# Attention on one NeuronCore: odd heads with exchanged query halves, key blocks in falling order, and a mask product over 512 columns

## Chip, cores and metric

One core of one Trainium2 chip. The metric is the device time of one execution in microseconds (us); the times of the kernel before are from three runs, and the median counts. The profile is of one further execution. Engines are named as in the profile: PE (matrix products; PEld is its weight load), DVE (vector), ACT (scalar), POOL (here stores and small memsets), SP (issues the loads).

## What is computed

One step of a small decoder: 1024 prompt positions and 8 decode positions, model width 2048. Layer A is a pooling mixer, then keys and values are projected once (4 key heads of 64), then layer B is sliding-window attention with 32 query heads of 64, a gate and an output projection. The change touches the attention of the prompt in layer B only:

```python
def attn_core(q, k, v, q_pos, k_pos, sinks):
    s = jnp.einsum('...qkgd,...skd->...kgqs', q, k).astype(jnp.float32) * (HEAD_DIM ** -0.5)
    ...
    mask = (kp <= qp) & (qp - kp < WINDOW) & (kp >= 0)
    s = jnp.where(mask[..., None, None, :, :], s, NEG)
    sink = sinks.astype(jnp.float32).reshape(N_KV_HEADS, GROUP)[:, :, None, None]
    m = jnp.maximum(jnp.max(s, axis=-1, keepdims=True), sink)
    p = jnp.exp(s - m)
    p = p / (jnp.sum(p, axis=-1, keepdims=True) + jnp.exp(sink - m))
    return jnp.einsum('...kgqs,...skd->...qkgd', p.astype(v.dtype), v)
```

With a window of 128, query q of a block of 128 sees keys 0 to q of its own block and keys q+1 to 127 of the block before, exactly 128 keys in all.

## The kernel before

**Staging.** The columns (positions) are worked in two chunks of 512 and 520, all of them in SBUF tiles of 128 x 1040 float32. 53 such slots (class `Mem`) are shared by everything: weights, activations, probabilities, gates. A slot is handed out whole (`full`) or in halves (`half`), the one that has been free longest first. Which slot a tile gets, and so whose last reader it must wait for, is thus settled when the program is built, by the order of the requests and of the frees; so is the place of a load, because activations and some sums are loaded ahead only while enough whole slots are free.

**Big products.** Input and output projections run as triples of PE products on numbers split into a high and a low part (lines 658 to 660, seven products for eight by sums of halves; lines 686 to 688, plain). A weight chunk is loaded by SP (line 287), ACT casts its high part (line 488), DVE subtracts for the low part (line 503) or forms sums of two chunks (lines 293 and 346). Activations (written to DRAM earlier and loaded at line 759) are cast at 769 and subtracted at 778. Partial sums are put away at 599 to 631.

**Order.** PE, DVE and ACT follow the order of the source (`in_order`). The big products of one phase are the steps; `product(n, rank, ...)` puts a smaller product between them, `at(n, ...)` puts other work n steps on. SP has one queue for all loads and runs it strictly in order: a load whose slot is still in use holds every later load. POOL issues the stores.

**Attention** (`attend`, lines 1745 to 1901) runs for 16 pairs of heads (j = 0, 1) in each of the two chunks, 32 times in all, as steps between the products of the input projection of layer B. Queries come from a rope step (lines 1616 to 1731: partner rows are fetched by four DMAs at 1616, added at 1624, finished at 1731). For a pair, with b the block of 128 queries in the chunk:

- score (line 1760): 32 PE products of 64 queries by 192 keys, in PSUM tile `pS`; query half u of block b goes to partitions u to u+63 and columns b*256+u on. The columns never written are zeroed once (`use_four`).
- select (ACT, 1778; in chunk 0 a POOL memset at 1776) copies the 128 columns of the block before into a slot; largest (DVE, 1782) overwrites them by `copy_predicated` with the scores of the own block where the key is not after the query, so that one row of 128 holds the whole window; then the row maxima (1786 to 1790).
- expo (ACT, 1797): eight activations of 128x128, one for each block and head, each summing its row; total (DVE, 1804 and 1805): the reciprocal; norm (ACT, 1810): eight activations of 128x128 that scale.
- turn (PE, 1814): eight transposes of 128x128 into PSUM; keep: ACT copies the 128x1024 result into slot `w` (1823) and DVE multiplies the same 128x1024 by a triangular mask of 0, 1 and -1 into slot `wp` (1824).
- values (PE, 1848): for each half k of the 64 keys a product of `w` with the values of one of the two blocks (64x128), and a correction of 64x64 with the difference of the two blocks' values on `wp`. The correction reads only the half of the columns of `wp` that belongs to query half k.
- gate (DVE, 1876), and a store by POOL.

## Time and profile before

| | us |
|---|---|
| median of 3 runs | 2360.77 (2357.7 to 2366.27) |
| profiled execution, its own time | 2356.38 |
| its span in the trace | 2354.6 |
| PE busy | 2297.3 |
| DVE busy | 1925.9 |
| ACT busy | 1343.1 |
| POOL busy | 205.5 |

The first attention step begins at 1157.9 us of the span and the last ends before 2060. A row of a group reads: line, engine, operation, output and input with their shapes, xcount | busy us, mean ns of one | idle us of the engine just before, and what ended that idle time. A row of waits reads: engine, tile and line that waited, the work it waited for, then us in total, how often, the longest.

### The profile page before, as it was taken

What the parts mean: (1) busy time and instruction counts of PE and PEld (TensorE: products, weight loads), DVE (VectorE), ACT (ScalarE), POOL (GpSimd) and SP (SyncE); (2) the same over time, 40 slices, a digit from 0 to 9 for tenths busy, and PEclk for the clock granted to TensorE, in tenths of its full rate; (3) what the DMA queues carried; (4) which work ended last, traced back from release to release, by engine and by line L of the source; (5) the groups of instructions that cost most, each with busy time, mean ns of one, the idle gap of its engine ahead of it and who ended that gap; (6) DMA issues with size and microseconds to landing.
All of it is one profiled execution on the core that took longest, in us unless ns stands there. A gap on an engine that the chain in (4) does not pass through costs nothing. (4 is left out here: it accounts for less than half of the span.)

```text
span 2354.6 us, 49710 instructions
## 1 busy us (share of the span) xinstructions
PE 2297.3 (98%) x19960; PEld 2200.9 (93%) x19960; DVE 1925.9 (82%) x2421; ACT 1343.1 (57%) x2429; POOL 205.5 (9%) x411
## 2 busy tenths in 40 slices
PE   8999999999999999999999899999999999999997
PEld 6899999999999999998788799999999999999997
DVE  8787998776878878978987788887777768888887
ACT  4444446544546547554465566685666678546556
POOL 0111110001000000000111111100000000000000
PEclk9999999999999999999999999999999999999999
DMA  8668789989889989999786766688777768799785
GB/s 293 211 246 303 271 299 346 332 292 319 289 289 339 327 280 333 328 388 327 272 310 220 248 219 239 224 310 270 237 249 245 230 201 305 239 342 372 260 300 199
DMA packets 250919, 665.18 MB, mean 283 GB/s; under 512 B 25632, under 2 KB 106432, under 8 KB 250688
## 3 DMA queue, kind: packets, MB, share of 16 engines
q1 hardware_dynamic: 205216, 496.94, 63.0%
q0 software_dynamic: 45472, 165.07, 18.1%
q8 instruction: 156, 2.56, 0.4%
q14 instruction: 75, 0.61, 0.1%
HBM read 466.81 MB, written 185.59 MB: 277 GB/s over the span
## 5 line engine op out<-in xcount | busy, mean ns | idle before, releaser
L658 PE MATMUL pD<-m,m 128*128 128x260 f32 (+1 forms) x4752 | 1346.0, 283 | 8.1 <-ACT pD L599 4.4
L660 PE MATMUL pD<-m,m 128*128 128x260 f32 (+1 forms) x4752 | 1339.1, 282 | 4.4 <-DVE m L503 4.4
L659 PE MATMUL pD<-m,m 128*128 128x260 f32 (+1 forms) x4752 | 1338.8, 282 | 0.0
L658 PEld LDWEIGHTS pD<-m,m 128*128 128x128 f32 x4752 | 894.5, 188 | 13.7 <-ACT pD L599 5.5
L660 PEld LDWEIGHTS pD<-m,m 128*128 128x128 f32 x4752 | 895.2, 188 | 5.5 <-DVE m L503 5.5
L503 DVE TENSOR_TENSOR m<-m,m 128x1024 fp32r<-128x1024 f32 x674 | 814.5, 1219 | 100.1 <-ACT m L488 60.6
L659 PEld LDWEIGHTS pD<-m,m 128*128 128x128 f32 x4752 | 894.9, 188 | 0.5
L488 ACT CAST m<-m 128x1024 fp32r<-128x1024 f32 x674 | 702.7, 1049 | 324.7 <-DVE m L346 85.1
L686 PE MATMUL pD<-m,m 128*128 128x512 f32 x448 | 179.7, 401 | 8.0 <-ACT m L769 8.0
L687 PE MATMUL pD<-m,m 128*128 128x512 f32 x448 | 177.9, 397 | 1.0 <-DVE m L778 1.0
L688 PE MATMUL pD<-m,m 128*128 128x512 f32 x448 | 177.5, 396 | 0.0
L778 DVE TENSOR_TENSOR m<-m,m 128x1024 fp32r<-128x1024 f32 (+1 forms) x120 | 147.0, 1226 | 6.4 <-ACT m L769 4.7
L769 ACT CAST m<-m 128x1024 fp32r<-128x1024 f32 (+1 forms) x120 | 125.9, 1053 | 17.7 <-PE pD L687 5.2
L631 ACT COPY m<-pD 128x260 f32<-128x260 f32 (+1 forms) x83 | 31.1, 375 | 179.2 <-PE pD L660 179.1
L346 DVE TENSOR_TENSOR m<-m,m 128x1024 f32<-128x1024 f32 x88 | 107.6, 1222 | 12.7 <-DMA m<-in_wib 6.3
L686 PEld LDWEIGHTS pD<-m,m 128*128 128x128 f32 x448 | 85.1, 190 | 28.1 <-ACT m L769 8.0
L687 PEld LDWEIGHTS pD<-m,m 128*128 128x128 f32 x448 | 85.0, 190 | 21.1 <-DVE m L778 2.1
L688 PEld LDWEIGHTS pD<-m,m 128*128 128x128 f32 x448 | 85.0, 190 | 19.7
L1797 ACT ACTIVATE m<-m,sm 128x128 f32<-128x128 f32 x256 | 99.4, 393 | 0.0
L619 DVE TENSOR_TENSOR m<-pD,m 128x260 f32<-128x260 f32 (+1 forms) x86 | 36.5, 424 | 74.4 <-PE pD L660 74.1
L1088 PE MATMUL pD<-m,m 128*128 128x260 f32 (+1 forms) x528 | 91.5, 323 | 0.0
L1088 PEld LDWEIGHTS pD<-m,m 128*128 128x128 f32 x528 | 79.5, 188 | 8.2
(249 smaller groups left out, 2180.9 us busy)
## 6 DMA issues: line engine op xcount, KB each, us to landing
m<-in_wia SPq DMA_DIRECT2D x124, 512.0 KB
m<-in_wib SPq DMA_DIRECT2D x120, 512.0 KB
swia<-m POOLq DMA_DIRECT2D x64, 512.0 KB, 4.8
m<-swia SPq DMA_DIRECT2D x64, 512.0 KB
m<-swoa SPq DMA_DIRECT2D x64, 512.0 KB
swib<-m POOLq DMA_DIRECT2D x64, 512.0 KB, 5.1
m<-swib SPq DMA_DIRECT2D x64, 512.0 KB
m<-swob SPq DMA_DIRECT2D x56, 512.0 KB
```

The lines of the kernel that those rows point to most:

```text
L346: self.nc.vector.tensor_add(s[out].a[:, :1024], s[x].a[:, :1024], s[y].a[:, :1024])
L488: self.nc.scalar.copy(hi.r[:, :1024], self.stream[self.cast].src().a[:, :1024])
L503: self.nc.vector.tensor_sub(lo.r[:, :1024], s.src().a[:, :1024], hi.a[:, :1024])
L658: nc.tensor.matmul(ps[:, :TH], wh[:, s], h, start=new and k == 0, stop=False, skip_group_check=on)
L659: nc.tensor.matmul(ps[:, :TH], wh[:, s], l, start=False, stop=False, skip_group_check=on)
L660: nc.tensor.matmul(ps[:, :TH], wl[:, s], h, start=False, stop=k == 7, skip_group_check=on)
L686: nc.tensor.matmul(ps[:], wh[:, s], h, start=par == 0 and k == 0, stop=False)
L687: nc.tensor.matmul(ps[:], wh[:, s], l, start=False, stop=False)
L688: nc.tensor.matmul(ps[:], wl[:, s], h, start=False, stop=par == 1 and k == 7)
L769: self.nc.scalar.copy(h.r[:, :n], s.a[:, :n])
L778: self.nc.vector.tensor_sub(l.r[:, :n], s.a[:, :n], h.a[:, :n])
L1088: nc.tensor.matmul(ps[:, : cs.stop - cs.start], ws[:, s], d[:, cs], start=f0 and k == 0, stop=l0 and k == 3,)
```

## The change

Which elements stand where is changed for the odd head of each pair, so that the two triangles that the correction needs lie in the same columns, one in partitions 0 to 63 and one in partitions 64 to 127.

- score: for j = 1 the two halves of 64 queries go to exchanged output partitions (z = 64-u). The 192 keys are read as three blocks of 64 in falling order, for both heads, so the own block lies in columns 0 to 127 of each 256 and the block before in 128 to 255. Number and shape of the products stay.
- select and largest take the other half of the columns; the mask of `copy_predicated` has a plane for each head, in bytes instead of 32-bit integers.
- norm: `wp` is now half a slot, taken at norm(0) instead of a whole slot at keep. The activations of blocks 0 and 7 are each cut in two of 64 columns, one of which writes into `wp`.
- turn: the transposes read 64 columns further on, so each result holds in its upper 64 partitions the second half of one block and in its lower 64 the first half of the next; the eighth reads the 128 columns in `wp`.
- keep: `w` as before; the product with the mask covers blocks 0 and 3 of each four, 512 columns, and is written over the same half slot `wp`.
- values: number and shape of the products stay; the index of the block of probabilities is turned by k, and for j = 1 the moving operand of the 64x128 products is read with its two halves exchanged.

```diff
-        self.mki = one.tile([P, P], I32, name="mki")
+        self.mki = one.tile([P, 2, P], U8, name="mki")
...
-                            self.S[u : u + 64, j, b * 256 + u : b * 256 + u + 192],
-                            q[r, b * P + u : b * P + u + 64],
-                            self.kT[t // 8][r, b * P + u : b * P + u + 192], start=True, stop=True,
+                            o.rearrange("p (m k) -> p m k", m=3), q[r, b * P + u : b * P + u + 64],
+                            k.rearrange("p (m k) -> p m k", m=3)[:, ::-1, :], start=True, stop=True,
...
-            nc.scalar.copy(s4[:, b0:], p4[:, b0:, :, 0:P])
+            nc.scalar.copy(s4[:, b0:], p4[:, b0:, :, P : 2 * P])
...
-                s4, self.mki[:, None, None, :].to_broadcast([P, NB, 2, P]), p4[:, :, :, P : 2 * P]
+                s4, self.mki[:, None, :, :].to_broadcast([P, NB, 2, P]), p4[:, :, :, 0:P]
...
+            if n == 0:
+                x["wp"] = self.mem.half()
             for i in range(4 * n, 4 * n + 4):
-                nc.scalar.activation(x["s3"][:, i, :], x["s3"][:, i, :], AF.Copy, scale=rs[:, i : i + 1])
+                v = x["s3"][:, i, :]
+                parts = [(v, v)]
+                if i in (0, 7):
+                    k1, k0 = v[:, :64], v[:, 64:]
+                    e = x["wp"].a[:, :P]
+                    parts = [(k0, k0), (e[:, 64:], k1)] if i == 0 else [(k1, k1), (e[:, :64], k0)]
+                for out, a in parts:
+                    nc.scalar.activation(out, a, AF.Copy, scale=rs[:, i : i + 1])
...
-                    PT[:, i * P : (i + 1) * P], x["sc"][:, i * P : (i + 1) * P], cst[:, K_ID : K_ID + P]
-                )
+                a = x["sc"][:, i * P + 64 : (i + 1) * P + 64] if i < 7 else x["wp"].a[:, :P]
+                nc.tensor.transpose(PT[:, i * P : (i + 1) * P], a, cst[:, K_ID : K_ID + P])
...
-            x["w"], x["wp"] = self.mem.full(), self.mem.full()
+            x["w"] = self.mem.full()
             nc.scalar.copy(x["w"].a[:, :1024], PT)
             nc.vector.tensor_mul(
-                x["wp"].a[:, :1024].rearrange("p (i k) -> p i k", k=P),
-                PT.rearrange("p (i k) -> p i k", k=P),
-                cst[:, None, K_MP : K_MP + P].to_broadcast([P, 8, P]),
+                x["wp"].a[:, :512].rearrange("p (b i k) -> p b i k", b=NB, i=2), mixed(slice(0, NB)),
+                cst[:, None, None, K_MP : K_MP + 64].to_broadcast([P, NB, 2, 64]),
             )
...
+                            i = (2 * b + j - k) % 8
...
+                                p = x["w"].a[r, i * P : i * P + P].rearrange("p (h q) -> p h q", h=2)
+                                if j:
+                                    p = p[:, ::-1, :]
```

**The order on SP.** Because `wp` is half a slot, most tiles after the first attention step get another slot, and some loads get another place in SP's queue. One place is the third phase of layer B's input projection, about 1300 to 1343 us in the trace of before. A row is line, DMA, slot with two running numbers <- DRAM tensor, shape; `in_wib` is the weight of layer B's input projection, `th0_92` an activation, line 1616 the rope partner rows. Before:

```order
L287 DMA m33_1722_14842<-in_wib 128x1024
L759 DMA m26_1729_14943<-th0_92 128x4x256
L287 DMA m45_1730_14945<-in_wib 128x1024
L759 DMA m2_1740_15039<-th0_92 128x4x256
L287 DMA m7_1731_14947<-in_wib 128x1024
L1616 DMA m40_1737_15030<-m43_1667_14239 32x512 x4
L759 DMA m50_1741_15041<-th0_92 128x4x256
L759 DMA m28_1747_15090<-th0_92 128x4x256
```

The same place after the change (line numbers are one higher there):

```order
L288 DMA m37_1718_14847<-in_wib 128x1024
L288 DMA m43_1724_14948<-in_wib 128x1024
L288 DMA m31_1725_14950<-in_wib 128x1024
L760 DMA m47_1734_15042<-th0_92 128x4x256
L760 DMA m0_1735_15044<-th0_92 128x4x256
L1617 DMA m33_1731_15033<-m3_1696_14596 32x512 x4
L760 DMA m9_1739_15090<-th0_92 128x4x256
L760 DMA m11_1740_15092<-th0_92 128x4x256
```

The three weight loads now stand together, and the two activation loads that stood between them follow behind.

**The order on ACT.** The place is the two norm steps of the first pair. `m_1605` is the slot with its probabilities, `sm` small vectors; 2050 to 2055 and 1908 (after: 2067 to 2072 and 1925) belong to the gate, 488 (489) is the cast of a weight. Before:

```order
L1810 ACTIVATE m_1605_13466<-m_1605_13466,sm_13487 128x128 x4
L2055 COPY m_1606_13496<-pD_13495 128x512
L1908 ACTIVATE m_1616_13600<-m_1606_13496 128x512
L488 CAST m_1619_13606<-m_1612_13552 128x1024
L1810 ACTIVATE m_1605_13466<-m_1605_13466,sm_13487 128x128 x4
```

After, where `m_1606` is `wp`:

```order
L1822 ACTIVATE m_1605_13466<-m_1605_13466,sm_13487 128x64
L1822 ACTIVATE m_1606_13496<-m_1605_13466,sm_13487 128x64
L1822 ACTIVATE m_1605_13466<-m_1605_13466,sm_13487 128x128 x3
L2072 COPY m_1589_13290<-pD_13495 128x512
L1925 ACTIVATE m_1616_13601<-m_1589_13290 128x512
L489 CAST m_1619_13607<-m_1612_13552 128x1024
L1822 ACTIVATE m_1605_13466<-m_1605_13466,sm_13487 128x128 x3
L1822 ACTIVATE m_1605_13466<-m_1605_13466,sm_13487 128x64
L1822 ACTIVATE m_1606_13496<-m_1605_13466,sm_13487 128x64
```

Each pair's norm has ten activations instead of eight, over the same columns. On PE the order of the rows stays as it was; on DVE the product with the mask keeps its place.

More of the change, by code (lines that the diff above doesn't have):

```diff
@@ L11 @@
 F32R = mybir.dt.float32r
-I32 = mybir.dt.int32
+U8 = mybir.dt.uint8
 AF = mybir.ActivationFunctionType
@@ L45 @@
 N_PRM = 116
-K_ID, K_MP, K_J, K_RC = 0, 128, 256, 384
-N_CST = 384 + 4 * NST
+K_ID, K_MP, K_J, K_RC = 0, 128, 192, 320
+N_CST = 320 + 4 * NST
 PHASES = (
@@ L248, in use_four @@
             for j in range(2):
-                self.nc.vector.memset(S4[64:, j, :, :64], 0.0)
-                self.nc.vector.memset(S4[:64, j, :, 192:], 0.0)
+                a, b = (slice(0, 64), slice(64, P))[:: 1 - 2 * j]
+                self.nc.vector.memset(S4[a, j, :, :64], 0.0)
+                self.nc.vector.memset(S4[b, j, :, 192:], 0.0)
     def psW(self):
@@ L1759, in score @@
                         r = slice(64 * j, 64 * j + 64)
+                        z = u if j == 0 else 64 - u
+                        o = self.S[z : z + 64, j, b * 256 + 64 - u : b * 256 + 256 - u]
+                        k = self.kT[t // 8][r, b * P + u : b * P + u + 192]
                         nc.tensor.matmul(
-                            self.S[u : u + 64, j, b * 256 + u : b * 256 + u + 192],
-                            q[r, b * P + u : b * P + u + 64],
-                            self.kT[t // 8][r, b * P + u : b * P + u + 192], start=True, stop=True,
+                            o.rearrange("p (m k) -> p m k", m=3), q[r, b * P + u : b * P + u + 64],
+                            k.rearrange("p (m k) -> p m k", m=3)[:, ::-1, :], start=True, stop=True,
                         )
@@ L1808, in norm, with mixed @@
             rs = x["sm"][3]
+            if n == 0:
+                x["wp"] = self.mem.half()
             for i in range(4 * n, 4 * n + 4):
-                nc.scalar.activation(x["s3"][:, i, :], x["s3"][:, i, :], AF.Copy, scale=rs[:, i : i + 1])
+                v = x["s3"][:, i, :]
[6 more added lines that the diff above has]
+                    nc.scalar.activation(out, a, AF.Copy, scale=rs[:, i : i + 1])
         def turn():
             for i in range(8):
-                nc.tensor.transpose(
-                    PT[:, i * P : (i + 1) * P], x["sc"][:, i * P : (i + 1) * P], cst[:, K_ID : K_ID + P]
-                )
+                a = x["sc"][:, i * P + 64 : (i + 1) * P + 64] if i < 7 else x["wp"].a[:, :P]
+                nc.tensor.transpose(PT[:, i * P : (i + 1) * P], a, cst[:, K_ID : K_ID + P])
             x["s"].free()
+        def mixed(b):
+            return PT.rearrange("p (b i k) -> p b i k", b=NB, i=4)[:, b, 0:4:3, :]
         def keep():
-            x["w"], x["wp"] = self.mem.full(), self.mem.full()
+            x["w"] = self.mem.full()
             nc.scalar.copy(x["w"].a[:, :1024], PT)
             nc.vector.tensor_mul(
-                x["wp"].a[:, :1024].rearrange("p (i k) -> p i k", k=P),
-                PT.rearrange("p (i k) -> p i k", k=P),
-                cst[:, None, K_MP : K_MP + P].to_broadcast([P, 8, P]),
+                x["wp"].a[:, :512].rearrange("p (b i k) -> p b i k", b=NB, i=2), mixed(slice(0, NB)),
+                cst[:, None, None, K_MP : K_MP + 64].to_broadcast([P, NB, 2, 64]),
             )
@@ L1842, in values @@
                         o = x["o"][b // 2]
-                        V, p = (self.Vd[b], x["wp"].a) if step else (self.V[b + 1 - k], x["w"].a)
-                        c0, c1 = (64 * k, 64 * k + 64) if step else (0, P)
+                        V = self.Vd[b] if step else self.V[b + 1 - k]
                         for j in range(2):
                             vs = slice((2 * (t // 8) + j) * HD, (2 * (t // 8) + j + 1) * HD)
-                            m = (2 * b + j) * P
+                            i = (2 * b + j - k) % 8
+                            out = o[64 * j : 64 * j + 64, n * P : (n + 1) * P].rearrange("p (h q) -> p h q", h=2)
+                            if step:
+                                out, p = out[:, k, :], x["wp"].a[r, i * 64 : i * 64 + 64]
+                            else:
+                                p = x["w"].a[r, i * P : i * P + P].rearrange("p (h q) -> p h q", h=2)
+                                if j:
+                                    p = p[:, ::-1, :]
                             ins = nc.tensor.matmul(
-                                o[64 * j : 64 * j + 64, n * P + c0 : n * P + c1], V[r, vs], p[r, m + c0 : m + c1],
+                                out, V[r, vs], p,
                                 start=part == 0 and n == 0 and step == 0, stop=part == 1 and step == 1,
@@ L2272, in _consts @@
     cst[:, K_ID : K_ID + P] = np.eye(P, dtype=f)
-    cst[:64, K_MP : K_MP + P] = i[:64, None] > i[None, :]
-    cst[64:, K_MP : K_MP + P] = -1.0 * (i[64:, None] <= i[None, :])
+    h = i[:64]
+    cst[:64, K_MP : K_MP + 64] = h[:, None] > h[None, :]
+    cst[64:, K_MP : K_MP + 64] = -1.0 * (h[:, None] <= h[None, :])
     cst[:, K_J : K_J + P] = 1.0 / D
@@ L2277, in _consts @@
         cst[:, K_RC + g * NST : K_RC + (g + 1) * NST] = w / np.minimum(w, np.arange(NST) + 1.0)
-    return cst, (i[None, :] <= i[:, None]).astype(np.int32)
+    k = (i + 64) % P
+    return cst, np.stack([k[None, :] <= q[:, None] for q in (i, k)], axis=1).astype(np.uint8)
 def kernel(**inputs):
```

## Prediction

> **What bounds the kernel now.** I read the page first, then the busy time by stretch, with the attention as the middle stretch.

> ```profile
> PE 2297.3 (98%) x19960; PEld 2200.9 (93%) x19960; DVE 1925.9 (82%) x2421; ACT 1343.1 (57%) x2429; POOL 205.5 (9%) x411
> 0.00:1157.00 1157.00, 1142.58 (x8696) 1099.72 (x8696) 952.38 (x1188) 580.42 (x822) 103.04 (x198) 1.00 0.86 304
> 1157.00:2060.00 903.00, 879.45 (x9019) 830.57 (x9020) 723.39 (x942) 587.99 (x1352) 85.01 (x185) 0.99 0.75 251
> ```

> The columns of a stretch are its us, then the busy us of PE, PEld, DVE, ACT and POOL, the granted PE clock, the DMA share and GB/s. PE is the bound: in the attention stretch it idles 903.0 - 879.5 = 23.5 us, while DVE idles 180 us and ACT 315 us. The change leaves number and shape of the PE products alone, so whatever it saves on DVE counts only where it shortens PE's 23.5 us of idle time, or the time PE ran at a lower clock. The next view is therefore what PE waits for in that stretch.

> ```profile
> PE pS L1760 <- DVE m L1731: 8.4, 8, 1.5
> PE pO L1848 <- ACT m L1823: 7.8, 1, 7.8
> PE pD L658 <- ACT pD L599: 1.8, 2, 0.9
> PE pS L1848 <- DVE m L1824: 1.5, 3, 0.7
> PE pD L660 <- DVE m L503: 1.3, 2, 1.1
> PE pD L1848 <- ACT m L614: 1.3, 1, 1.3
> PE pO L1848 <- DVE m L1824: 0.6, 1, 0.6
> ```

> Only two rows, 1.5 + 0.6 us, name the product with the mask, which is what the change shortens. The two large ones are the scores that wait for the rope step, and one single wait of 7.8 us. I followed that one back in time, engine by engine.

> ```profile
> 1311.58 0.38 SPq L759 DMA_DIRECT2D m<-th  x1
> 1312.06 0.45 SPq L287 DMA_DIRECT2D m<-in_wib  x1
> 1320.25 0.38 SPq L759 DMA_DIRECT2D m<-th  x1
> 1320.73 0.99 SPq L287 DMA_DIRECT2D m<-in_wib  x1
> SPq L759 <- DMA swib<-m: 7.7, 1, 7.7
> 1321.97 1.22 DVE L503 TENSOR_TENSOR m<-m,m 128x1024 fp32r<-128x1024 f32 x1
> 1328.94 1.22 DVE L346 TENSOR_TENSOR m<-m,m 128x1024 f32<-128x1024 f32 x1 [5.75 <-DMA m<-in_wib]
> 1330.20 1.04 ACT L488 CAST m<-m 128x1024 fp32r<-128x1024 f32 x1 [9.02 <-DVE m L346]
> 1333.73 1.00 ACT L1823 COPY m<-pS 128x1024 f32<-128x1024 f32 x1
> 1326.60 0.40 PE L688 MATMUL pD<-m,m 128*128 128x512 f32 x1
> 1334.79 0.48 PE L1848 MATMUL pO<-m,m 64*64 64x128 f32 x2 [7.79 <-ACT m L1823]
> 1336.05 0.37 PE L1848 MATMUL pO<-m,m 64*64 64x64 f32 x2 [0.55 <-DVE m L1824]
> ```

> On SP an activation load (759) stood 7.7 us until a store out of its slot (`swib`) was done, and held the weight load behind it until 1320.73. DVE had nothing to do from 1323.19 until the weight came (5.75 us), added it at 1328.94; ACT, which keeps the order of the source, stood at the cast of that sum and so came to the copy of the probabilities (1823) only at 1333.73; PE stood 7.79 us. The wait is put down to ACT, but its root is a load that came late. It also cost clock, in the windows around it:

> ```profile
> 1320.00:1327.00 7.00, 7.00 (x35) 5.45 (x33) 3.09 (x5) 0.59 (x1) 0.11 (x1) 1.00 0.97 298
> 1327.00:1335.00 8.00, 0.21 (x4) 0.21 (x8) 3.73 (x4) 4.80 (x14) 1.07 (x2) 0.71 0.98 269
> 1335.00:1341.00 6.00, 5.45 (x42) 4.15 (x39) 5.97 (x6) 2.23 (x9) 0.70 (x3) 0.53 0.95 302
> 1341.00:1350.00 9.00, 9.00 (x88) 8.00 (x87) 8.86 (x16) 7.50 (x15) 2.09 (x4) 1.00 0.85 319
> ```

> The granted clock was 0.53 from 1335 to 1341, just when PE had work again: 6.0 x (1 - 0.53) = 2.8 us more. So this one stall is worth 7.8 + 0.55 + 2.8 = 11 us.

> [...]

> **The change part by part.** First the product with the mask.

> ```profile
> L1824 DVE TENSOR_TENSOR m<-pS,cst 128x1024 f32<-128x1024 f32 x32 | 39.2, 1225 | 57.2 <-ACT m L1823 46.5 <-PE pD L659 9.0 <-ACT m L1810 1.8
> L1731 DVE TENSOR_TENSOR m<-m,m 128x512 f32<-128x512 f32 x8 | 5.5, 692 | 0.3
> 1820.74 1.23 DVE L1824 TENSOR_TENSOR m<-pS,cst 128x1024 f32<-128x1024 f32 x1 [0.91 <-ACT m L1823]
> 1822.13 2.39 DVE L1624 TENSOR_TENSOR m<-m,m 128x1040 f32<-128x1040 f32 x2
> 1824.56 1.24 DVE L1731 TENSOR_TENSOR m<-m,m 128x1040 f32<-128x1040 f32 x1
> 1481.23 1.22 DVE L1731 TENSOR_TENSOR m<-m,m 128x1024 f32<-128x1024 f32 x1
> L1624 DVE TENSOR_TENSOR m<-m,m 128x1040 f32<-128x1040 f32 x18 | 21.5, 1236 | 6.8 <-DMA m<-m 6.8
> L1782 DVE COPY_PREDICATED m<-mki,pS 128x1024 f32<-128x1024 int32 x32 | 42.2, 1320 | 0.0
> ```

> 1225 ns for 1024 columns and 692 ns for 512 give 0.53 us a pair, 32 x 0.53 = 17 us of DVE's busy time (the 512 columns are no longer in one piece in PSUM; nothing here shows a price for that). It cannot be 17 us of time: the mask product itself was preceded by 57.2 us of idle time, 46.5 of them for ACT's copy. What reaches PE is this. The values waits on 1824: four, 2.1 us, three of them in the 1.5 us row, of which at most 0.53 each can go: -1.3. The score waits on 1731: where DVE runs mask product, two rope adds and 1731 without a gap (the rows at 1820.74 to 1824.56 are one place; the 1731 at 1481.23 ends another such run, and there is a third at 1432), the 0.53 us come through whole: three times, -1.6. The other five of the eight are held by the partner rows' DMA (6.8 us of idle time before 1624). SP's queue before several of those DMAs moves forward in the changed order; between 0 and -3, I take -1.

> Second the slots. With `wp` as half a slot, the third phase's three weight loads stand together ahead of the two activations. Following the slots to their last readers: the second and third weights of the group take slots whose last readers are the PE products (686 to 688) that end with the activation load's own wait at 1311.58. So both should be issued by about 1312, 9 us sooner than 1320.73. The load took at most 1328.94 - 1320.73 = 8.2 us to land; from 1312 that is 1320.2, before DVE is free at 1323.19. DVE's sum then moves forward by the whole 5.75 us, ACT's copy behind it too, and PE's wait falls from 7.79 to about 2.0 us. At 2 us I expect no drop of the clock: PE's other waits here are at most 1.5 us, and none shows one. With the 0.55 mostly gone: -5.75 - 2.8 - 0.3 = -8.9 us. What is late next there is the ACT chain from the cast to the copy, unchanged. Ends: -5.7 if the clock still drops, -11 if the whole stall goes. What was pushed back, the activation loads and the sums that wait for spare slots, comes later by 6 to 65 us, and with before's times each still lands 6 us or more ahead of its use; that is the cover, and if one misses it, a wait like the one above returns (a rival).

> Third ACT's pieces.

> ```profile
> 1308.38 1.28 ACT L1810 ACTIVATE m<-m,sm 128x128 f32<-128x128 f32 x4
> L1810 ACT ACTIVATE m<-m,sm 128x128 f32<-128x128 f32 x256 | 82.3, 399 | 6.1 <-DVE sm L1805 6.1
> 1331.15 0.20 ACT L1795 ACTIVATE sm<-sm 128x8 f32<-128x8 f32 x1
> L1814 PE MATMUL pS<-cst,m x256: 270/272/274, 1200.4 to 2027.8; 128*128 128x128 f32 x128
> ```

> Four pieces take 1.28 us, so they follow (1.28 - 0.40) / 3 = 0.29 us apart. A piece of 64 columns lies between 128 x 8 (0.20 us long) and 128 x 128 (0.40), about 0.1 shorter than the latter: 0.19 apart. Two more pieces a pair then cost 4 x 0.19 - 2 x 0.29 = 0.18 us, 32 times 6 us; at the ends 0 (two halves cost as much as a whole) and 0.58 x 32 = 19 us. The cover is ACT's 315 idle us, and the transposes, which wait for norm, appear nowhere among PE's waits. New is that norm(0) waits for its half slot; `select` of another pair, casts and copies queue behind it. Where the slot has just been read by a product, I find three such waits of about 1.4 us, before idle stretches of ACT. I take +1 for all this, ends 0 and +5.

> [...]

> Fourth, PE's own products: same number, shapes and order. The moving operands are now read in pieces of 64 columns in falling order, which no row of before shows. I take nothing, since the columns within a piece stay in rising order; the price if that is wrong is a rival. `copy_predicated` with a byte mask reads less; it could be quicker than its 1.32 us (mean of the 32), and is hidden either way, as no PE wait names it. The memsets and constants are done once.

> Fifth, every slot after the first pair is another, so small waits come and go elsewhere: between -2 and +5, I take +1.

> Sum: -1.3 - 1.6 - 1 - 8.9 + 1 + 1 = -10.8, about -11 us. The profiled run took 2356.4 us (span 2354.6 and 1.8 around it), so it would take 2345.4. The median of the three runs is 4.4 us above the profiled one; on its scale the forecast is 2360.8 - 10.8 = 2350.

> **The rivals.**

> (a) The saving lies beside other work, and the stall stays or returns elsewhere as another late load. For it: 46.5 us of DVE's idle time is for ACT's copy, so the mask product is rarely late, and the sums for the next phase do move later. Against it: the order shows the very load moved ahead. It leaves -1.3 - 1.6 and up to +2: -1 to -4, so 2357 to 2360.

> (b) More goes than I count: the whole stall (11), all 8.4 us of score waits that DMA or DVE hold, and the values waits: -11 - 6 to 8 - 2 = -19 to -21, so 2340 to 2342. For it: DVE, which is ahead by up to 17 us in sum, releases slots sooner. Against it: the ACT chain at the stall, 4.5 us from cast to copy, is not shortened.

> (c) Slower: the moving operands in falling pieces of 64 columns are read more slowly. The place is score, and values for odd heads.

> ```profile
> 1351.14 1.53 PE L1760 MATMUL pS<-m,m 64*64 64x192 f32 x32
> ```

> Were each pass twice as long, a score would cost about 1.5 us more, 32 x 1.5 = 48 us all on PE, so 2350 + 48 = 2398. It decides from a lengthening of 23% on: 32 x 0.35 = 11 us eats the gain. Nothing in the trace speaks for it, nothing excludes it. A second way to this side, the half slot held from norm(0) on, which would bring an activation late enough for a stall of 11 us on top of the one that is there, would give 2369; I count it with (a), as still under 0.5%.

> (d) The change does not save what it says: 512 columns in two pieces of 128 for each block cost DVE as much as 1024. That only takes away 1.3 + 1.6: 2353.

> **How the numbers follow.** A measurement of this kernel can tell about 0.5% from no change, 11.8 us: faster is under 2349.0, slower over 2372.6. My forecast of -11 with its terms' ends (-6 to -15, with d in it) has a chance of 0.62, half on each side of 2349; (a) 0.20; (b) 0.12; (c) 0.06. Faster: 0.31 + 0.12 = 0.43; within: 0.31 + 0.20 = 0.51; slower: 0.06. The range goes from (b)'s 2340 to (a)'s 2360, with 1 us for the medians; it leaves out (c) and the tails of the others, 0.15 or so.

> **What would show it.** Right: SP issues the three weight loads of that place by about 1312; PE's wait there is near 2 us and the clock stays at 1.00; the mask product takes 0.69 us; DVE's busy time falls by 17 us while the span falls by 11; PE's busy time stays within 3 us (its half-clock stretch) of 2297; ACT's rises by 6. Wrong: a new PE wait of more than 3 us in 1157 to 2060, a score of over 1.6 us, or a second stretch of lower clock.

## The result

The median went from 2358.07 us to 2346.02 us, six runs each: a ratio of 0.9945, with a 95% interval of 0.9930 to 0.9961. That is 12 us less; the forecast was 10.8 us less, and 2350 on the scale of the three runs shown then. The profiled execution took 2346.26 us, its span is 2344.4 us, 10.2 less than before.

The busy times of the changed kernel, from its page:

```profile
PE 2297.8 (98%) x19960; PEld 2202.2 (94%) x19960; DVE 1908.6 (81%) x2421; ACT 1353.3 (58%) x2493; POOL 205.2 (9%) x411
```

DVE has 17.3 us less, ACT 10.2 more (64 more activations), PE the same. What PE waits for in the attention stretch, of the changed kernel (columns: us in total, times, longest):

```profile
PE pS L1764 <- DVE m L1732: 3.4, 4, 1.5
PE pD L661 <- DVE m L504: 2.2, 4, 1.2
PE pO L1865 <- ACT m L1835: 1.9, 1, 1.9
PE pD L659 <- DVE m L620: 1.4, 1, 1.4
PE pD L1865 <- POOL flag L1873: 1.1, 3, 0.8
PE pD L1865 <- ACT m L615: 0.9, 1, 0.9
PE pS L1865 <- DVE m L1836: 0.4, 2, 0.2
PE pO L1865 <- DVE m L1836: 0.3, 1, 0.3
```

The single wait of 7.8 us for ACT's copy is 1.9 us, the score waits (8.4 us) are 3.4, the values' waits on the mask product (2.1) are 0.7. The place of the old stall, in the changed kernel's timeline of SP, DVE, ACT and PE:

```profile
1306.04 7.22 SPq L288 DMA_DIRECT2D m<-in_wib  x3
1313.37 8.83 SPq L760 DMA_DIRECT2D m<-th  x2
1323.63 1.22 DVE L347 TENSOR_TENSOR m<-m,m 128x1024 f32<-128x1024 f32 x1
1324.88 1.05 ACT L489 CAST m<-m 128x1024 fp32r<-128x1024 f32 x1 [3.05 <-DVE m L347]
1328.42 1.00 ACT L1835 COPY m<-pS 128x1024 f32<-128x1024 f32 x1
1329.48 0.33 PE L1865 MATMUL pO<-m,m 64*64 64x128 f32 x2 [1.88 <-ACT m L1835]
1330.20 0.27 PE L1865 MATMUL pO<-m,m 64*64 64x64 f32 x2 [0.28 <-DVE m L1836]
```

The three weight loads are issued by 1313.3, DVE adds without a wait, the same chain of ACT (cast at 1324.88 to copy at 1328.42) follows 5.3 us sooner. The activation load still stands some 8 us behind its store on SP, but nothing urgent is queued behind it. One thing is not as forecast, in stretches of 3.41 us:

```profile
357.90:361.31 3.41, 1.47 (x13) 1.26 (x12) 3.41 (x4) 3.38 (x6) 0.00 (x0) 1.00 0.92 279
361.31:364.72 3.41, 3.41 (x17) 3.41 (x18) 3.38 (x4) 3.02 (x4) 0.53 (x1) 0.50 1.07 388
1327.28:1330.69 3.41, 1.26 (x34) 0.69 (x32) 1.23 (x2) 3.41 (x11) 0.00 (x0) 1.00 1.03 356
1330.69:1334.11 3.42, 3.42 (x20) 2.63 (x13) 3.42 (x4) 1.22 (x3) 0.64 (x2) 0.50 1.03 388
```

The clock (the number behind the five engines) fell to 0.50 for one stretch after a wait of 1.88 us. So it did at 361 us too, long before the attention, where the profiled run of before kept its clock. The first score of after starts 1.4 us later than that of before, and from there to the end it gains 11.6 us.

### The profile page after: what moved, and what is told of

Read it like the earlier page. It is cut to its first block, busy times and chain, and to the rows that moved or that the text cites. A ratio compares the mean times of both kernels' runs of the same rounds, so it can differ in the third digit from the quotient of the medians.

```text
span 2344.4 us, 49741 instructions
## 1 busy us (share of the span) xinstructions
PE 2297.8 (98%) x19960; PEld 2202.2 (94%) x19960; DVE 1908.6 (81%) x2421; ACT 1353.3 (58%) x2493; POOL 205.2 (9%) x411
## 5 line engine op out<-in xcount | busy, mean ns | idle before, releaser
L659 PE MATMUL pD<-m,m 128*128 128x260 f32 (+1 forms) x4752 | 1347.2, 283 | 8.6 <-DVE m L620 5.2
L660 PE MATMUL pD<-m,m 128*128 128x260 f32 (+1 forms) x4752 | 1339.6, 282 | 0.0
L659 PEld LDWEIGHTS pD<-m,m 128*128 128x128 f32 x4752 | 895.2, 188 | 14.1 <-ACT pD L600 4.3
L661 PEld LDWEIGHTS pD<-m,m 128*128 128x128 f32 x4752 | 896.0, 189 | 7.2 <-DVE m L504 7.1
L660 PEld LDWEIGHTS pD<-m,m 128*128 128x128 f32 x4752 | 895.7, 188 | 0.5
L688 PE MATMUL pD<-m,m 128*128 128x512 f32 x448 | 177.7, 397 | 0.9 <-DVE m L779 0.9
L687 PEld LDWEIGHTS pD<-m,m 128*128 128x128 f32 x448 | 85.1, 190 | 28.1 <-ACT m L770 8.1
L688 PEld LDWEIGHTS pD<-m,m 128*128 128x128 f32 x448 | 85.1, 190 | 21.0 <-DVE m L779 2.0
L689 PEld LDWEIGHTS pD<-m,m 128*128 128x128 f32 x448 | 84.9, 189 | 19.7
L1822 ACT ACTIVATE m<-m,sm 128x128 f32<-128x128 f32 (+1 forms) x320 | 94.2, 372 | 8.3 <-DVE sm L1808 5.9
```

Of the source, the lines that this page charges most:

```text
L659: nc.tensor.matmul(ps[:, :TH], wh[:, s], h, start=new and k == 0, stop=False, skip_group_check=on)
L660: nc.tensor.matmul(ps[:, :TH], wh[:, s], l, start=False, stop=False, skip_group_check=on)
L661: nc.tensor.matmul(ps[:, :TH], wl[:, s], h, start=False, stop=k == 7, skip_group_check=on)
L687: nc.tensor.matmul(ps[:], wh[:, s], h, start=par == 0 and k == 0, stop=False)
L688: nc.tensor.matmul(ps[:], wh[:, s], l, start=False, stop=False)
L689: nc.tensor.matmul(ps[:], wl[:, s], h, start=False, stop=par == 1 and k == 7)
```

## The experiments

The theory on record (A): the gain is the late weight load, worth most of it, plus a few small waits on the mask product. The rival (B): it is DVE's 17 us of work. Ratios are to the kernel before, run alongside, with 95% intervals; us are medians. Each kernel has one trace, so what the rows show is one execution each. Line numbers in rows are those of the kernel that the run was made from, or a few higher.

**Loads moved alone.** The kernel before; an activation load is not issued in the steps between the weight loads.

```diff
-            if self.xl and n < X_AGE + 2 and (free() > spare + ...
+            if not 428 < self.i < 433 and self.xl and n < X_AGE + 2 and (free() > spare + ...
```

> The kernel before with one condition more: the activation load that stood between the three weight loads of the third phase is not issued until three steps later. No instruction is shortened. Theory A (the gain is the late weight load): the 7.8 us wait of PE at the values there falls to about 2 us, and the time falls by 7 to 9 us of the 12, to about 2350. Theory B (the gain is DVE's 17 us): nothing of DVE's work is gone, so at most 1 us goes, 2357.

Measured: 2351.9, ratio 0.9970 (0.9960 to 0.9980), 6 to 7 us. Its PE waits:

```profile
PE pS L1760 <- DVE m L1731: 6.8, 9, 1.5
PE pD L658 <- ACT m L1797: 2.7, 1, 2.7
PE pO L1848 <- ACT m L1823: 1.8, 1, 1.8
```

The old wait is 1.8 us, as in the changed kernel: the load alone does that. But 30 us later there is a new one of 2.7 us, put down to ACT's exponentials, and the clock halves after it:

```profile
1358.58:1361.99 3.41, 0.68 (x7) 0.59 (x6) 3.41 (x5) 2.60 (x9) 0.53 (x1) 1.00 0.64 215
1361.99:1365.41 3.42, 3.42 (x19) 3.42 (x18) 3.39 (x5) 0.52 (x1) 0.73 (x2) 0.50 0.35 143
```

DVE is busy in the whole of both stretches (3.41 and 3.39 us). It puts away partial sums (619) until 0.14 us before PE goes on, and the same product waits 1.4 us for that operation in the changed kernel (the row with 620 above). So the wait is more likely DVE's, which works off here what it no longer waited for at the stall, than ACT's; no run separates the two. Comparing starts of equal steps, the stall gave 8.1 us and this place took 4.4 back. The moved load also exchanges other loads of SP's queue at ten later places.

**Mask product alone.** The kernel before, slots and queues unchanged, the product over the first 512 columns in place; half of the correction is left out.

```diff
-                x["wp"].a[:, :1024].rearrange("p (i k) -> p i k", k=P),
-                PT.rearrange("p (i k) -> p i k", k=P),
-                cst[:, None, K_MP : K_MP + P].to_broadcast([P, 8, P]),
+                x["wp"].a[:, :512].rearrange("p (i k) -> p i k", k=P),
+                PT[:, :512].rearrange("p (i k) -> p i k", k=P),
+                cst[:, None, K_MP : K_MP + P].to_broadcast([P, 4, P]),
```

> The kernel before with the mask product over the first 512 columns only, in place, and the corrections reading those; half of the correction is left out, the slots and the order of every queue stay as before. Theory A: the 7.8 us wait stays, the three score waits and the values waits on the mask product shrink by 2 to 3.5 us in sum, 2355. Theory B: DVE's busy time falls by 17 us and 9 to 12 us of time go with it, 2347.

Measured: 2348.9, ratio 0.9960 (0.9948 to 0.9972): 9 us, between the two theories and nearer to B. Its PE waits:

```profile
PE pO L1849 <- ACT m L1823: 8.3, 1, 8.3
PE pS L1760 <- DVE m L1731: 3.7, 6, 1.5
PE pS L1849 <- DVE m L1824: 0.3, 1, 0.3
```

The stall stays, as A has it, but the score waits fall by 4.7 us and not by the 1.6 that A gave DVE. The queue of SP has the same loads in the same places (but for one pair of neighbours exchanged), so the order of the loads is not what ended the score waits that I had put down to the partner rows' DMA. That the shorter product ended them is not shown either: with the loads moved, where the product is whole, most of the same waits are gone too (the table further down).

**Mask product twice, in the changed kernel.** The same product is issued a second time, and SP's queue keeps its order. DVE gets back more than the change took away: its 64 mask products are busy 44.3 us (692 ns each), 22.2 more than the 32 of the changed kernel (22.1) and 5.1 more than those of before (39.2), since two of them take 1.38 us where the one of before took 1.23.

```diff
-            nc.vector.tensor_mul(
+            for _ in range(2):
+                nc.vector.tensor_mul(
```

> The changed kernel with the product with the mask issued twice, the second over the first: DVE gets its 17 to 18 us back, all slots and all other queues stay. Theory A: 2 to 4 us are lost, 2348 to 2350. Theory B: about 10 us are lost, 2356.

Measured: 2360.1, ratio 1.0006 (0.9997 to 1.0014): 14 us, the whole gain and a little more, are gone, loads in their good places or not. Theory A in its first form falls. B had 2356; as the dose is larger than what was taken away, the 14 us are no measure of those 17 us of DVE. Its PE waits, to be set beside those of the changed kernel above:

```profile
PE pS L1764 <- DVE m L1732: 4.9, 6, 2.0
PE pD L1866 <- POOL flag L1874: 2.9, 6, 0.8
PE pS L1866 <- DVE m L1837: 2.2, 4, 1.0
PE pD L1866 <- ACT m L615: 2.0, 1, 2.0
PE pO L1866 <- DVE m L1837: 1.0, 1, 1.0
```

These are 13.0 us where the changed kernel has 3.4 + 1.1 + 0.4 + 0.9 + 0.3 = 6.1, so 6.9 more; and two of them have grown to 2.0 us. Behind the first, that on 615, the clock is at half for a stretch:

```profile
1524.40:1527.81 3.41, 1.41 (x35) 1.03 (x33) 3.26 (x3) 2.11 (x3) 0.31 (x1) 1.00 1.08 370
1527.81:1531.22 3.41, 3.21 (x46) 2.46 (x46) 3.41 (x5) 3.41 (x9) 0.10 (x1) 0.50 1.04 380
```

The other stands before a score, at 1825.9 in the table further down; its clock is in no row here, but the mean granted clock of the profiled run is 0.995 where the changed kernel's is 0.997. If it cost the same, two such stretches of 3.41 us at half clock are 2 x 1.7 = 3.4 us, an estimate. Together 10.3 of the 12.4 us between the two profiled runs (2358.6 and 2346.3).

**Load put back, in the changed kernel.** The one activation load is issued at its old step.

```diff
-            if self.xl and n < X_AGE + 2 and (free() > spare + ...
+            if self.xl and n < X_AGE + 2 and (self.i == 430 and self.xl[0] == (1, 1) or free() > spare + ...
```

> The changed kernel with one activation load issued at the step where it was before, between the weight loads of the third phase; the mask product stays at 512 columns. Theory A: a PE wait of 6 to 8 us at the values there and the longer stretch of lower clock come back, 7 to 9 us are lost, 2353 to 2355. Theory B: nothing changes, 2346.

Measured: 2351.9, ratio 0.9970 (0.9957 to 0.9983), 6 us of the gain lost. SP, DVE and the wait of PE there:

```profile
1322.74 0.38 SPq L760 DMA_DIRECT2D m<-th  x1
1323.29 0.47 SPq L288 DMA_DIRECT2D m<-in_wib  x1
1330.87 1.22 DVE L347 TENSOR_TENSOR m<-m,m 128x1024 f32<-128x1024 f32 x1 [6.08 <-DMA m<-in_wib]
PE pO L1865 <- ACT m L1835: 7.5, 1, 7.5
```

The rows of before are back, by one load's place, and the mean granted clock of the profiled run is 0.995, where the changed kernel has 0.997 and the kernel before 0.996. That mechanism is shown from both sides; put back, the load costs 6 of the 12 us, and comparing starts of equal steps, 5.6 of them are lost at this place.

**Both parts on the kernel before**, without half slots and cut pieces (half of the correction left out): the two edits of the first two runs together.

> The kernel before with the loads moved as in the first run and the mask product over 512 columns as in the second (half of the correction left out), without half slots and cut pieces. If the two parts add, 7 + 9 us go, 2342, and the change itself gives back 4 us elsewhere; if they overlap, it is 2346, like the changed kernel.

Measured: 2348.4, ratio 0.9958 (0.9941 to 0.9974). The parts do not add: 6 and 9 us apart, 9 or 10 together. Its PE waits:

```profile
PE pS L1760 <- DVE m L1731: 6.9, 8, 2.4
PE pO L1849 <- ACT m L1823: 1.8, 1, 1.8
```

The stall is 1.8, but the score waits are 6.9 and not 3.7 us. The waits right before a score's first product, place by place (us; places by their start in the kernel before; the first two, at 1158.0 and 1182.1, are 1.5 and 0.2 in every run):

| run | 1433.7 | 1482.5 | 1628.7 | 1723.9 | 1774.7 | 1825.9 |
|---|---|---|---|---|---|---|
| before | 1.14 | 1.15 | 1.52 | 0.84 | 1.48 | 0.63 |
| loads moved alone | 1.11 | 1.18 | 0.58 | 0 | 0.20 | 0.95 |
| mask product alone | 0.61 | 0.62 | 0 | 0.22 | 0.14 | 0.57 |
| both | 0.58 | 0.64 | 2.38 | 0 | 0 | 1.11 |
| changed | 0 | 0 | 0 | 0 | 0.09 | 1.29 |
| changed, mask twice | 0 | 0 | 0 | 0 | 0.82 | 2.00 |

At 1628.7, 1723.9 and 1774.7 the rope adds of the kernel before wait for the partner rows' DMA (DVE idles 3.86, 1.02 and 1.65 us). One of these places, in the kernel before and with the loads moved alone:

```profile
1771.01 2.40 DVE L1624 TENSOR_TENSOR m<-m,m 128x1040 f32<-128x1040 f32 x2 [1.65 <-DMA m<-m]
1774.74 1.53 PE L1760 MATMUL pS<-m,m 64*64 64x192 f32 x32 [1.48 <-DVE m L1731]
1765.89 2.40 DVE L1624 TENSOR_TENSOR m<-m,m 128x1040 f32<-128x1040 f32 x2 [0.39 <-DMA m<-m]
1769.62 1.53 PE L1760 MATMUL pS<-m,m 64*64 64x192 f32 x32 [0.20 <-DVE m L1731]
```

In sum the three waits are 3.8 us before, 0.8 with the loads moved and 0.4 with the mask product alone. Both runs thus count the same 3 us and more as a gain, and together they keep 1.5 of it, as 2.4 us of it are back at 1628.7. By these traces that is most of what is missing from 6 + 9. It also says that these waits do not hang on the mask product's length alone; only at 1433.7 and 1482.5 does a wait shrink by its 0.53 us and stay when the loads alone are moved.

The interval overlaps that of the change (0.9930 to 0.9961), so the rest of the change, half slots, other order and cut pieces, costs or gains nothing that these runs resolve.

**ACT's pieces: all eight blocks cut**, in the changed kernel.

```diff
-                parts = [(v, v)]
+                parts = [(v[:, :64], v[:, :64]), (v[:, 64:], v[:, 64:])]
```

> The changed kernel with all eight norm blocks of a pair cut in two pieces of 64 columns, not two of them; only ACT gets more work, 6 pieces of about 0.19 us a pair, 36 us in all, four queues stay. If ACT's pieces reach PE (a tenth of them or more already in the change), 4 to 10 us are lost, 2350 to 2356. If they lie in ACT's idle time, as the prediction has it, at most 2 us, 2348.

Measured: 2344.4, ratio 0.9944 (0.9929 to 0.9958), the same as the change, with ACT 31 us busier:

```profile
PE 2296.5 (98%) x19960; PEld 2201.0 (94%) x19960; DVE 1908.1 (81%) x2421; ACT 1384.5 (59%) x2685; POOL 205.3 (9%) x411
```

**The pieces on the mask run of before**: two blocks cut in place (half of the correction left out).

> The kernel before with the mask product over 512 columns (half of the correction left out) and two of the eight norm blocks cut in place in pieces of 64 columns: against the run with the mask product alone, only ACT's pieces are new, about 12 us on ACT. If they are what the change gives back, 3 to 4 us are lost, 2352; if not, within 1 us of 2349.

Measured: 2351.6, ratio 0.9975 (0.9965 to 0.9986) against 0.9960 (0.9948 to 0.9972) without the pieces: 3 us by the medians, though the intervals overlap.

**The pieces on the run with the loads moved**, mask product whole.

> The kernel before with the loads moved (the first run, 2352) and two of the eight norm blocks cut in place in two pieces. The mask product is whole. Two ways to explain that the changed kernel with its mask product doubled is 8 us slower than the first run: if ACT's cut pieces cost time as long as DVE is not relieved, this run takes 2357 to 2360; if it is the changed order of slots and loads, it stays within 2 us of 2352.

Measured: 2353.2, ratio 0.9973 (0.9962 to 0.9985): within 2 us of the 2351.9 without them.

**Mask twice, norm uncut**, and **norm uncut** in the changed kernel; the last block is written whole into the half slot.

```diff
-                if i in (0, 7):
-                    k1, k0 = v[:, :64], v[:, 64:]
-                    e = x["wp"].a[:, :P]
-                    parts = [(k0, k0), (e[:, 64:], k1)] if i == 0 else [(k1, k1), (e[:, :64], k0)]
+                if i == 7:
+                    parts = [(x["wp"].a[:, :P], v)]
```

> The changed kernel with the mask product issued twice, and norm in eight whole pieces, the last of them written into the half slot (the output is wrong by two half blocks a pair). If ACT's cut pieces cost 6 to 8 us there, this takes 2352 to 2354; if it is the order, 2358 to 2361 as with the pieces.

> The changed kernel with norm in eight whole pieces, the last written into the half slot (the output is wrong by two half blocks a pair), the mask product once: what the cut pieces cost in the change itself. If they are hidden, 2344 to 2347 as with them; if they are not, 2342 or less.

Measured: 2358.0, ratio 0.9997 (0.9987 to 1.0006), and 2342.9, ratio 0.9933 (0.9918 to 0.9947). So the pieces cost 2 to 3 us by the medians in either, inside the intervals (the second run lies between the two times that were expected of it). They are not why the doubled product costs 14 us; without them it costs 15. With the doubled product the changed order takes 2360, or 2358 without the pieces, where the order of before with the loads moved takes 2352. Part of that can be the dose, as with the pieces the two mask products are 5.1 us busier (44.3) than the one in the run with the loads moved (39.2); how much is the order's is not shown.

**Copy and mask product a step earlier** (five pairs of the changed kernel).

```diff
-            self.at(at + s1, lambda: self.posts.append(keep))
+            self.at(at + s1, keep)
```

> The changed kernel with ACT's copy and the mask product of five pairs issued in the step of their transposes and not at the start of the next, so that at the place of the old stall the copy stands ahead of four exponentials and a cast. The slots after that pair change again. Expected there: PE's wait falls from 1.9 to under 0.5 us and the clock stays up, 3 to 4 us less, 2342; the rival is that new slots bring a wait elsewhere of 2 us or more, 2345 to 2348.

Measured: 2347.2, ratio 0.9955 (0.9941 to 0.9969), the rival of its expectation. At the old place PE no longer waits at all and the clock stays up (its products of 512 columns take 0.39 us there, where in the changed kernel they took 0.63 at half clock), but its waits elsewhere grew, and the mean granted clock of the profiled run is 0.997, as in the changed kernel:

```profile
PE pD L1865 <- ACT m L615: 2.8, 1, 2.8
PE pD L659 <- DVE m L620: 2.3, 1, 2.3
PE pD L659 <- DVE m L1893: 1.5, 1, 1.5
```

**5 us of other DVE work taken away**, the small subtraction of the sink, in the changed kernel.

```diff
-            nc.vector.tensor_tensor(v3(es), v3(nm), nsk, op=ALU.subtract)
...
-                nc.scalar.activation(es[:], es[:], AF.Exp)
+                for j in range(2):
+                    o, a = (v[:].rearrange("p (b j) -> p b j", j=2)[:, :, j] for v in (es, nm))
+                    k = C_SINK + 2 * t + j
+                    nc.scalar.activation(o, a, AF.Exp, bias=self.prm[:, k : k + 1])
```

> The changed kernel with one small DVE operation a pair less: the subtraction of the sink from the negated maximum (0.17 us, 32 times, 5.4 us of DVE) is folded into the bias of two activations instead of one; ACT gets 32 small activations more, about 4 us. All slots, loads and the other queues stay. If DVE's time is worth in this order what the doubled mask product showed, 0.7 us per us, 3 to 5 us go, 2342; if the doubled product cost so much only because it stands right ahead of the values and the rope, at most 1 us, 2345 to 2346.

Measured: 2345.8, ratio 0.9948 (0.9934 to 0.9962), no change, with DVE 5 us less busy:

```profile
PE 2298.6 (98%) x19960; PEld 2202.3 (94%) x19960; DVE 1903.6 (81%) x2389; ACT 1360.9 (58%) x2525; POOL 205.6 (9%) x411
```

That points to the place of DVE's work and not its amount, but does not show it. At the rate of the doubled product (14 us for 22.2) the 5 us would be worth 3, which the intervals do not exclude, and ACT is 7.6 us busier. The mask product differs from the subtraction by its place: it starts right behind ACT's copy (in the changed kernel DVE idles 54.5 us for it, before 30 of the 32), and right behind it on DVE stand the rope step and what the next products need. No version tried beats the changed kernel beyond the intervals.

## Why the prediction was right in sum, and where not

- **The stall.** Right in its mechanism and its size on PE: the loads came when they were to, the wait fell to 1.88 us (forecast 2.0), the runs with the load moved and put back show the cause. Its term was -8.9; comparing starts of equal steps before and behind the place, it gave 7.3. The failed step is "At 2 us I expect no drop of the clock", argued from waits of at most 1.5 us: one stretch of 3.41 us ran at half after the wait of 1.88 us, by estimate 1.7 us.
- **Values waits on the mask product.** Forecast -1.3, measured 2.1 to 0.7, -1.4. The mask product takes 692 ns, as taken from another operation of that width:

```profile
L1836 DVE TENSOR_TENSOR m<-pS,cst x32: 682/692/693, 1205.0 to 2021.2; 128x512 f32<-128x512 f32 x32
L1785 DVE COPY_PREDICATED m<-mki,pS x32: 1305/1319/1336, 1167.1 to 1992.3; 128x1024 f32<-128x1024 uint8 x32
```

 The two pieces of a block in PSUM cost nothing extra (692 ns too with the mask product alone, whose 512 columns are in one piece), and the byte mask gains nothing (1319 ns, 1317 before).
- **Score waits.** This term was mis-sized: -1.6 for DVE and -1 for the loads, measured -5.0. "Three times, -1.6" came true at two places only with the mask product alone (0.53 each at 1433.7 and 1482.5, nothing at 1825.9). "Held by the partner rows' DMA" was right for three of the other five, and there nearly all of the 3.8 us went, not 1; the first two, 1.5 and 0.2 us, have no such idle time before their rope adds and never changed. Even with the product doubled, which makes it longer than before, the changed kernel keeps 3.5 of the 5.0. So in the changed kernel most of this term goes with the order of slots and loads, for which -1 was taken. Why the three waits also shrink in the old order, with the mask product alone, was not settled.
- **ACT's pieces.** Forecast +6 us of ACT, hidden; ACT rose by 10.2, and half a pair's norm takes 1.47 us where it took 1.28, so 0.38 a pair and not 0.18:

```profile
1336.99 1.47 ACT L1822 ACTIVATE m<-m,sm 128x64 f32<-128x64 f32 x5
L1822 ACT ACTIVATE m<-m,sm 128x64 f32<-128x64 f32 x128 | 37.6, 342 | 8.3 <-DVE sm L1808 5.9 <-PE pD L660 2.5
```

 The mis-sized step is "0.19 apart": with all blocks cut, eight pieces take 2.03 us and a piece by itself 0.34, so they follow (2.03 - 0.34) / 7 = 0.24 us apart.

```profile
1307.59 2.03 ACT L1822 ACTIVATE m<-m,sm 128x64 f32<-128x64 f32 x8
```

 From start to start whole blocks are 0.29 us apart, so the pieces gain less by their width than was taken; by themselves a piece lasts 342 ns and a block 393. That the pieces are hidden stands as far as the runs resolve: 31 us more of ACT changed nothing, the runs without pieces are 2 to 3 us faster inside the intervals.
- **Reversed operands and other slots.** The score products take 323 ns as before, so rival (c) is out. New small waits came (1.4 us on 620, 0.9 more on 504), about the +1 to +2 taken.
- **The sum.** -10.8 was met by -12 because the stall gave 1.6 less and the score waits 2.4 more: two misses that went against each other, and that is luck. What the working did not see is that the terms are not independent: 6 us and 9 us measured alone make 9 to 10 together on the old order, mostly because both lose the same score waits, and in the new order 22 us more of DVE in that one place cost 14. That about 6 of the 12 us hang on the load is shown by putting it back; how the rest divides between the order and the mask product stays open.

## What to carry to other kernels

Follow the longest single wait back through every queue that runs in order before pricing the operation that is edited; here one load behind another in SP's queue was worth 6 of the 12 us, and a change of a buffer's size moved it. Look at what is queued right behind an operation on its engine, and not only at its share of busy time: 22 us more of DVE between ACT's copy and the rope cost 14 us, while 5 us less elsewhere on the same engine showed nothing, though the runs do not quite separate place from amount. Gains measured one at a time don't add where two edits remove the same waits: compare the waits place by place before adding the times.

## What the hardware showed

```profile
357.58:361.00 3.42, 1.51 (x13) 1.30 (x12) 3.42 (x4) 3.39 (x7) 0.00 (x0) 1.00 0.92 286
361.00:364.40 3.40, 3.36 (x28) 3.37 (x29) 3.37 (x4) 3.27 (x5) 0.53 (x1) 1.00 1.06 368
```

The wait itself is the same in both traces, 1.95 us before and 1.94 after. Its last few hundredths lay in the next stretch in the one, and it lay wholly in one stretch in the other, where 3.41 us at half clock followed, products of 256 columns took 0.41 us and not 0.28, and the first score came 1.4 us later. So one and the same wait cost 1.9 us in one trace and some 1.4 more in the other, at a place that the change does not touch; and the wait on 615, which grew from 0.9 to 2.0 us with the doubled product, cost more than it grew, as the rows at 1524.40 and 1527.81 show. How much idle time it takes, and whether its place in the raster decides, these few stretches don't settle.
